# Attention weights normalised before they are transposed, a sink as a score column, and full-size products in filters and values

## The chip, the cores and the metric

The kernel runs on one core of a Trainium2 chip. Its time is the device time of one execution, in microseconds. Inputs and output lie in the device's main memory (HBM). The engines of the core are TensorE (PE; its weight loads are listed apart as PEld), VectorE (DVE), ScalarE (ACT), GpSimd (POOL) and SyncE (SP, which issues most DMAs). Each engine runs its own instructions in the order that was fixed when the program was built, and waits where an operand isn't ready.

## The reference, cut to what matters

A first block (retention, mLSTM and a feed-forward network over 512 tokens of width 1024) is followed by four layers: a latent attention, a windowed attention with a sink, a layer of long convolutions, and a second latent attention. There are 512 tokens and 256 context tokens; the last layer gives no context output. The change touches the softmax of the three attentions, and the convolutions' filters:

```python
def dense_attend(q, k, v, scale):            # latent attention, 8 heads
    s = jnp.einsum('bqhd,bkhd->bhqk', q, k).astype(jnp.float32) * scale
    p = jax.nn.softmax(s, axis=-1).astype(v.dtype)
    return jnp.einsum('bhqk,bkhd->bqhd', p, v)
...
def sink_attend(scores, values, sink_l):     # windowed attention, 16 heads in 4 groups
    sink_col = jnp.broadcast_to(sink_l[None, :, :, None, None], scores[0].shape[:-1] + (1,))
    p = jax.nn.softmax(jnp.concatenate(scores + [sink_col], axis=-1), axis=-1)
...
    y_x = (o_x * jax.nn.silu(gate_x)) @ w_out
...
def hyena_filters(n, f_w1, f_b1, f_freq, f_w2, f_b2, f_w3):
    h = jnp.sin(freq * (z @ f_w1 + f_b1))
    h = jnp.sin(freq * (h @ f_w2 + f_b2))
    h = (h @ f_w3).astype(jnp.float32).reshape(n, 2, C_ORDER, C_WIDTH)
    return h * jnp.exp(-t[:, :, None, None] * deltas)
```

## The kernel before, in words

All tensors lie with features on the 128 partitions and tokens along the columns. Precision beyond one pass of TensorE comes from splitting: `split` (line 396) writes a rounded high part with ScalarE and the remainder, the low part, with VectorE, and `mac` (line 436) multiplies high by high, high by low and low by high into one PSUM bank. Three products therefore stand for one.

The text of the kernel is a set of Python generators, which `weave` and `mix` interleave by given weights. That gives the written order; each engine's own order, fixed at build time, follows it closely, but takes an instruction ahead where an earlier one would wait. Tiles come from pools with a fixed number of buffers: four PSUM banks (`mm`), two double banks (`mm2`), eight tiles of 768 columns for softmax weights and other things (`P`), four of each small tag. A tile's next user waits for its last reader.

**The softmax** (line 1376) runs with queries on the partitions. VectorE takes the maximum of a row of scores in PSUM (line 1380), a one-column operation makes the exponential's bias of it (1382, or 1384 with the sink), ScalarE writes the exponentials `P` to SBUF and adds them up (1385), and VectorE takes the reciprocal of the sum into a column of `rd` (1389). With a sink, ScalarE also takes the sink's exponential (1387), which is added to the sum (1388). `P` stays unnormalised. The scale of the scores is a factor of the exponential.

**The latent attention** (`mla`) makes for each head 4 score tiles of 128 queries by 768 keys (`stageA`, line 1570), and in its first layer also 2 tiles of 128 context queries by 256 context keys. `stageB` (line 1590) goes over the blocks of 128 keys: `transposed` (line 1391) turns the block of all query tiles on TensorE (line 1395), splits the result, and `mac` multiplies it with the values one block later. At the end `over_columns` (line 1369) transposes each column of `rd`, broadcast to 128 columns, against the identity, so that 1/sum stands along the columns on all partitions (line 1373); VectorE multiplies it with the gate (1605) and with the output (1606). While `stageB` of one head runs, `stageA` of the next one and the preparation of later heads are woven in.

**The windowed attention** (`swa`) has 24 units (4 groups of heads; 2 context and 4 token tiles each). A unit's `stageA` (line 1703) makes the scores of its 4 heads: context keys, and a band of 2 or 3 blocks on which a mask is added by a product. `stageB` of the unit before is mixed in. Its values are stored with their high and low parts side by side, 64 columns each; `transposed` gives the weights' parts. A product of all 128 columns with the high weights (line 1739) gives two halves of the result, and one of the 64 high columns with the low weights (1738 or 1741) adds to the first half. ScalarE copies the transposed 1/sum with the factor 0.5 (1744), VectorE multiplies (1745), adds the two halves (1749) and applies the gate (1752).

**The filters** (`filter_unit`, line 1855) are made during the first block's feed-forward network (line 1156). The hidden layer `hv` has its high part in rows 0 to 63 and its low part in rows 64 to 127; the weights `w` repeat their high part in both halves. So line 1873 gives two of the three terms in one product with 128 rows; line 1874 adds the third with the 64 rows of the high part and the 64 rows of the low weights `l`. There are 48 such pairs.

**Queries**: `stacks` (line 1361) splits two halves of 64 rows so that high and low part of one head fill 128 rows; `split` does the same for the latent attention's 128-row queries.

Of the kernel before, what the change touches and what calls it, by code (L numbers as in the profile page):

```python
# [19 lines left out]
N = 512  # L20
# [234 lines left out]
class Kern:  # L255
# [140 lines left out]
    def split(self, dst, src):  # L396
        self.nc.scalar.copy(dst.hi, src)  # L397
        self.nc.vector.tensor_tensor(dst.lo, src, dst.hi.bitcast(F32), ALU.subtract)  # L398
# [962 lines left out]
    def stacks(self, r, n, d0, d1):  # L1361

        nc = self.nc
        nc.scalar.copy(d0[0:64, :], r[0:64, :])
        nc.vector.tensor_tensor(d0[64:128, :], r[0:64, :], d0[0:64, :].bitcast(F32), ALU.subtract)
        nc.scalar.copy(d1[64:128, :], r[64:128, :])
        nc.vector.tensor_tensor(d1[0:64, :], r[64:128, :], d1[64:128, :].bitcast(F32), ALU.subtract)
# [8 lines left out]
    def softmax(self, S, P, rd, scale, sink=None):  # L1376

        nc = self.nc
        s = self.sp.tile([128, 8], F32, tag="sm", name="sm")
        nc.vector.tensor_reduce(s[:, 0:1], S, AX.X, ALU.max)  # L1380
        if sink is None:
            nc.vector.tensor_scalar(s[:, 1:2], s[:, 0:1], -scale, None, ALU.mult)  # L1382
        else:
            nc.vector.tensor_scalar(s[:, 1:2], s[:, 0:1], -scale, sink[1], ALU.mult, ALU.min)
        nc.scalar.activation(P, S, AF.Exp, bias=s[:, 1:2], scale=scale, accum_out=s[:, 2:3])  # L1385
        if sink is not None:
            nc.scalar.activation(s[:, 3:4], sink[0], AF.Exp, bias=s[:, 1:2])
            nc.vector.tensor_tensor(s[:, 2:3], s[:, 2:3], s[:, 3:4], ALU.add)
        nc.vector.reciprocal(rd, s[:, 2:3])
# [48 lines left out]
    def mla(self, j, ctx_out, bg, end):  # L1438
# [107 lines left out]
        def queries(hp):  # L1546
            rp = self.wslot(4, 128)
            qs = [[self.b(dt=F32R), self.b(dt=F32R)], None]
            if ctx_out:
                t = self.b(dt=F32R)  # L1550
                qs[1] = [t[:, 0:256], t[:, 256:512]]
            for u in range(2):
                raw = self.wload(Wq, 0, 4, 384 * hp + 192 * u, 192)
                t = self.wslot(4, 128)
                self.split(rp[:, :, 64 * u:64 * u + 64], raw[:, :, 128:192])
                self.split(t, raw[:, :, 0:128])
                o = H[2 * hp + u]
                o["qs"] = [x[u] if x else None for x in qs]
                for i, n in ((0, N), (1, NC))[:2 if ctx_out else 1]:
                    q = self.bhl(n)  # L1560
                    self.split(q, self.proj([t[:, k, :] for k in range(4)], qn[i], n))
                    o["q"].append(q)
                yield
            rp = [rp[:, k, :] for k in range(4)]
            self.stacks(self.rope64(self.proj(rp, qn[0], N)), N, *qs[0])
            if ctx_out:
                self.stacks(self.proj(rp, qn[1], NC), NC, *qs[1])
            yield

        def stageA(h, i):  # L1570

            o = H[h]
            n = (N, NC)[i]
            o["P", i], o["rd", i] = [], self.sp.tile([128, 4], F32, tag="rd", name="rd")
            for qt in range(n // 128):
                sl = slice(128 * qt, 128 * qt + 128)
                ps = self.mm2() if i == 0 else self.mm()
                off = 256 if i == 0 else 0
                for x in (1, 0)[:2 - i]:
                    dst = ps[:, 512:1024] if x == 0 else ps[:, off:off + 256]  # L1580
                    self.mac(dst, [(o["q"][i][:, sl], o["k"][x])], stop=False)
                    nc.tensor.matmul(dst, o["qs"][i][:, sl], kr[x].hi, start=False, stop=False)  # L1582
                    nc.tensor.matmul(dst, o["qs"][i][:, sl], kr[x].lo, start=False, stop=True)  # L1583
                tot = 768 if i == 0 else 256
                P = self.P(tot)
                self.softmax(ps[:, off:off + tot], P, o["rd", i][:, qt:qt + 1], scale)
                o["P", i].append(P)
                yield

        def stageB(h, i):  # L1590
# [13 lines left out]
            rd = o["rd", i]  # L1604
            nc.vector.tensor_tensor(g, self.over_columns([rd[:, x:x + 1] for x in range(n // 128)], 128), g, ALU.mult)
# [23 lines left out]
    def swa(self, bg, end):  # L1629
# [5 lines left out]
        nsink = self.c2.tile([128, 16], F32, name="nsink")  # L1635
        nc.vector.tensor_scalar(nsink, self.sink, -1.0, None, ALU.mult)
# [32 lines left out]
        def queries(g, u, i):  # L1669
            def f(ps):  # L1670
# [6 lines left out]
                self.stacks(self.rope64(ps) if i == 0 else ps, ns[i], *gq[g, i][2 * u:2 * u + 2])  # L1677
# [25 lines left out]
        def stageA(g, i, qt):  # L1703
# [4 lines left out]
            rd = self.sp.tile([128, 4], F32, tag="rd", name="rd")  # L1708
            for v in range(4):
                ps = self.mm2()  # L1710
                q = gq[g, i][v][:, sl]
# [13 lines left out]
            U[g, i, qt] = (Ps, rd, list(range(k0, k1)) + [4, 5], sl)  # L1725

        def stageB(g, i, qt):
            Ps, rd, blocks, sl = U.pop((g, i, qt))
# [17 lines left out]
            ov = rb.rearrange("p (h q) -> p h q", h=4)  # L1746
            o = self.t(256)
            for v in range(2):
                nc.vector.tensor_tensor(o[64 * v:64 * v + 64, :].rearrange("p (h q) -> p h q", h=2), ov[0:64, v::2, :], ov[64:128, v::2, :], ALU.add)
            yield  # L1750
            for u in range(2):
                nc.vector.tensor_tensor(o[:, 128 * u:128 * u + 128], o[:, 128 * u:128 * u + 128], gs[g, i][u][:, sl], ALU.mult)
# [8 lines left out]
        def attend(some):  # L1761

            for x in some:
                n = units.index(x)
                prev = units[n - 1] if n else None
                yield from mix((stageA(*x), 4), (stageB(*prev), len(U[prev][2]) + 2) if prev else (None, 1))
# [68 lines left out]
    def filter_head(self, cg, o):  # L1835
# [8 lines left out]
        for op in (ALU.add, ALU.subtract):  # L1844
# [7 lines left out]
            ws.append((w, l[0:64, :]))  # L1852
        return dl, ws

    def filter_unit(self, cg, o, dl, ws):

        nc, I = self.nc, self.I
        for i, nt in ((0, 2), (1, 1)):
            hv = self.fh[i].rearrange("p (t q) -> p q t", q=2)
            for wi, (w, l) in enumerate(ws):  # L1860
# [8 lines left out]
                for par in range(2):  # L1869
                    for t in range(nt):  # L1870
# [3 lines left out]
                        nc.tensor.matmul(ps, x[0:64, :], l, start=False, stop=True)  # L1874
# [231 lines left out]
```

## Time and profile before

| | |
|---|---|
| time, median of 3 runs | 2917.35 us (2915.61 to 2918.12) |
| profiled execution: its own time / span of its instructions | 2918.76 us / 2917.0 us |
| granted clock of TensorE, mean over the span | 0.982 of full |
| TensorE busy (matmuls) | 2787.1 us, 96% |
| VectorE, ScalarE, GpSimd busy | 1814.9, 1334.4, 128.8 us |
| instructions | 44103, of them 17106 matmuls |

Busy time is the union of an engine's instructions. Matmuls overlap in their records, so a matmul's recorded length (some 0.39 us for 512 columns) is longer than the distance to the next one's start. A row of the view by group gives the line of the kernel, the engine and operation, what is written and read, the shape, the count, then the busy time and the mean length in ns, and behind the last bar the idle time before these instructions with what ended it. In the view in order of time a row gives the start and the length in us; "xN" merges neighbours of one kind.

### The profile page before, as it was taken

The numbers are of one execution on the slowest core, as the hardware profiler recorded it, in microseconds if no ns is written. First come the engines' busy times: TensorE is split into PE (matmuls) and PEld (weight loads), VectorE is DVE, ScalarE is ACT, GpSimd is POOL, SyncE is SP. The second block draws the span as 40 slices with busy tenths as digits, with TensorE's granted clock in tenths as the row PEclk, the third lists the DMA queues.
The fourth block names the chain that finished last, engine by engine and source line by source line (L and its number), as shares of the span: only waits on it lengthen the run. The fifth ranks groups of instructions, "written<-read, shape, count | busy, mean of one in ns | idle before, by whom it ended". The sixth has DMA issues, their size and how long they took to land. (4 is left out here: it accounts for less than half of the span.)

```text
span 2917.0 us, 44103 instructions
## 1 busy us (share of the span) xinstructions
PE 2787.1 (96%) x17106; PEld 2364.2 (81%) x17106; DVE 1814.9 (62%) x3775; ACT 1334.4 (46%) x2610; POOL 128.8 (4%) x158
## 2 busy tenths in 40 slices
PE   7999999999999999999999999989999998999998
PEld 4888878887777787888889877778888886887887
DVE  6665455555655556246768577788576777754774
ACT  4344344346455433345555566675332223544553
POOL 1000000000000000000000000000021122000000
PEclk8999999999999999999999999999999999999998
DMA  7233232544555536321234241123132226432122
GB/s 264 86 111 123 73 101 84 168 154 141 164 158 163 170 112 209 108 67 44 68 93 156 64 131 42 35 71 117 62 95 84 84 80 195 130 97 63 56 82 69
DMA packets 365830, 318.98 MB, mean 109 GB/s; under 512 B 17511, under 2 KB 326517, under 8 KB 365620
## 3 DMA queue, kind: packets, MB, share of 16 engines
q1 hardware_dynamic: 365204, 315.99, 35.2%
q8 instruction: 134, 2.20, 0.3%
q14 instruction: 76, 0.62, 0.1%
q0 software_dynamic: 416, 0.17, 0.0%
HBM read 273.90 MB, written 42.21 MB: 108 GB/s over the span
## 5 line engine op out<-in xcount | busy, mean ns | idle before, releaser
L441 PE MATMUL mm<-b,whi 128*128 128x512 f32 (+1 forms) x2548 | 895.8, 352 | 4.7 <-ACT whi L397 2.5
L443 PE MATMUL mm<-b,wlo 128*128 128x512 f32 (+1 forms) x2548 | 887.3, 348 | 1.2 <-DVE wlo L398 1.1
L442 PE MATMUL mm<-b,whi 128*128 128x512 f32 (+1 forms) x2548 | 887.6, 348 | 0.0
L441 PEld LDWEIGHTS mm<-b,whi 128*128 128x128 f32 x2548 | 486.1, 191 | 74.4 <-issue 5.8
L443 PEld LDWEIGHTS mm<-b,wlo 128*128 128x128 f32 x2548 | 486.1, 191 | 62.0 <-DVE wlo L398 2.3
L442 PEld LDWEIGHTS mm<-b,whi 128*128 128x128 f32 x2548 | 486.5, 191 | 60.2 <-issue 0.8
L398 DVE TENSOR_TENSOR wlo<-raw,whi 128x1024 fp32r<-128x1024 f32 (+3 forms) x286 | 292.0, 1023 | 239.7 <-ACT whi L397 224.1
L397 ACT CAST whi<-raw 128x1024 fp32r<-128x1024 f32 (+3 forms) x286 | 252.3, 885 | 397.1 <-PE mm L442 253.9
L443 PE MATMUL mm<-b 128*128 128x256 f32 (+1 forms) x628 | 189.4, 302 | 0.5 <-DVE b L398 0.3
L1385 ACT ACTIVATE P<-mm,sm 128x768 f32<-128x768 f32 (+3 forms) x176 | 127.9, 727 | 116.6 <-DVE sm L1382 68.4
L441 PE MATMUL mm<-b 128*128 128x256 f32 (+1 forms) x500 | 158.2, 318 | 8.4 <-ACT P L1385 4.6
L441 PE MATMUL mm<-b,P 128*128 128x256 f32 x560 | 161.8, 289 | 4.0 <-ACT b L575 2.8
L442 PE MATMUL mm<-b,P 128*128 128x256 f32 x560 | 160.4, 286 | 0.9 <-DVE b L576 0.8
L442 PE MATMUL mm<-b 128*128 128x256 f32 (+1 forms) x500 | 153.0, 307 | 0.4 <-DVE b L398 0.3
L1380 DVE TENSOR_REDUCE sm<-mm 128x1 f32<-128x768 f32 (+3 forms) x176 | 128.6, 733 | 39.7 <-PE mm L1583 23.8
L245 POOL TENSOR_TENSOR rs<-rs,mhalf 128x2 f32<-128x2 f32 (+1 forms) x44 | 42.3, 962 | 2427.2 <-DVE rs L244 2279.8
L398 DVE TENSOR_TENSOR t<-mm,t 128x512 fp32r<-128x512 f32 (+1 forms) x208 | 136.5, 663 | 15.3 <-ACT t L397 14.1
L397 ACT CAST t<-mm 128x512 fp32r<-128x512 f32 (+1 forms) x208 | 116.0, 569 | 54.8 <-PE mm L1395 51.6
L235 DVE TENSOR_TENSOR t<-t 128x256 f32<-128x256 f32 (+1 forms) x216 | 92.5, 441 | 71.9 <-ACT t L231 69.4
L1395 PE MATMUL mm<-ct,P 128*128 128x128 f32 x768 | 122.8, 276 | 13.0 <-ACT P L1385 8.2
L231 ACT ACTIVATE t<-b 128x256 f32<-128x256 f32 (+1 forms) x252 | 100.7, 431 | 67.7 <-DVE b L1101 40.9
L443 PEld LDWEIGHTS mm<-b 128*128 128x128 f32 x628 | 120.6, 192 | 5.6 <-DVE b L398 1.3
(351 smaller groups left out, 5129.7 us busy)
## 6 DMA issues: line engine op xcount, KB each, us to landing
raw<-in_w_mod_dram SPq DMA_DIRECT2D x96, 512.0 KB, 4.4
raw<-in_w_ada_dram SPq DMA_DIRECT2D x48, 512.0 KB, 3.9
raw<-in_w_in_dram SPq DMA_DIRECT2D x48, 512.0 KB, 4.0
raw<-in_w_ffn_in_dram SPq DMA_DIRECT2D x44, 512.0 KB, 4.1
raw<-in_c_w_in_dram SPq DMA_DIRECT2D x32, 512.0 KB, 4.3
raw<-in_a_w_in_dram SPq DMA_DIRECT2D x28, 512.0 KB, 4.1
ks<-t SPq DMA_DIRECT2D x48, 256.0 KB, 2.8
raw<-ks SPq DMA_DIRECT2D x24, 512.0 KB, 3.3
```

The costliest lines, as they stand in the source:

```text
L231: self.k.nc.scalar.activation(sq, x, AF.Square)
L235: self.k.nc.vector.tensor_tensor(self.acc, self.acc, sq, ALU.add)
L245: nc.gpsimd.tensor_tensor(s[:, 4:4 + nt], s[:, :nt], self.k.mhalf[:, :nt], ALU.pow)
L397: self.nc.scalar.copy(dst.hi, src)
L398: self.nc.vector.tensor_tensor(dst.lo, src, dst.hi.bitcast(F32), ALU.subtract)
L441: nc.tensor.matmul(ps, l.hi, r.hi, start=start and i == 0, stop=False)
L442: nc.tensor.matmul(ps, l.hi, r.lo, start=False, stop=False)
L443: nc.tensor.matmul(ps, l.lo, r.hi, start=False, stop=stop and i == n - 1)
L1380: nc.vector.tensor_reduce(s[:, 0:1], S, AX.X, ALU.max)
L1385: nc.scalar.activation(P, S, AF.Exp, bias=s[:, 1:2], scale=scale, accum_out=s[:, 2:3])
L1395: self.nc.tensor.transpose(ps[:, 128 * i:128 * i + 128], b, self.ident)
```

## The change

The softmax's weights are multiplied by 1/sum on GpSimd, in place, before they are transposed; `rd`, the transposes of its columns and the multiplications behind them go. The scale is multiplied into the queries when they are split. The sink becomes one more column of the scores, written into PSUM by ScalarE ahead of the head's score products, so that maximum, exponential and sum take it in; the column isn't transposed. In the windowed attention the low weights are multiplied with all 128 columns of the values. In the filters the low weights get 64 rows of zeros, and the product takes all 128 rows.

```diff
-    def split(self, dst, src):
-        self.nc.scalar.copy(dst.hi, src)
-        self.nc.vector.tensor_tensor(dst.lo, src, dst.hi.bitcast(F32), ALU.subtract)
+    def split(self, dst, src, scale=None):
...
+            nc.scalar.activation(dst.hi, src, AF.Copy, scale=scale)
+            nc.vector.scalar_tensor_tensor(dst.lo, src, scale, dst.hi.bitcast(F32), ALU.mult, ALU.subtract)
...
-    def softmax(self, S, P, rd, scale, sink=None):
+    def softmax(self, S, P, keep):
         nc = self.nc
-        s = self.sp.tile([128, 8], F32, tag="sm", name="sm")
-        nc.vector.tensor_reduce(s[:, 0:1], S, AX.X, ALU.max)
-        if sink is None:
-            nc.vector.tensor_scalar(s[:, 1:2], s[:, 0:1], -scale, None, ALU.mult)
-        else:
-            nc.vector.tensor_scalar(s[:, 1:2], s[:, 0:1], -scale, sink[1], ALU.mult, ALU.min)
-        nc.scalar.activation(P, S, AF.Exp, bias=s[:, 1:2], scale=scale, accum_out=s[:, 2:3])
-        if sink is not None:
-            nc.scalar.activation(s[:, 3:4], sink[0], AF.Exp, bias=s[:, 1:2])
-            nc.vector.tensor_tensor(s[:, 2:3], s[:, 2:3], s[:, 3:4], ALU.add)
-        nc.vector.reciprocal(rd, s[:, 2:3])
+        s = self.sp.tile([128, 4], F32, tag="sm", name="sm")
+        nc.vector.tensor_reduce(s[:, 0:1], S, AX.X, ALU.max, negate=True)
+        nc.scalar.activation(P, S, AF.Exp, bias=s[:, 0:1], accum_out=s[:, 1:2])
+        nc.vector.reciprocal(s[:, 2:3], s[:, 1:2])
+        nc.gpsimd.tensor_scalar(P[:, :keep], P[:, :keep], s[:, 2:3], None, ALU.mult)
...
-            rd = o["rd", i]
-            nc.vector.tensor_tensor(g, self.over_columns([rd[:, x:x + 1] for x in range(n // 128)], 128), g, ALU.mult)
             nc.vector.tensor_tensor(g, out, g, ALU.mult)
...
+                h = 4 * g + v
+                nc.scalar.copy(ps[:, 768:769], self.sink[:, h:h + 1])
...
-                P = self.P(nb + 256)
-                h = 4 * g + v
-                self.softmax(ps[:, 512 - nb:768], P, rd[:, v:v + 1], scale, (self.sink[:, h:h + 1], nsink[:, h:h + 1]))
+                P = self.P(nb + 257)
+                self.softmax(ps[:, 512 - nb:769], P, nb + 256)
...
-                    last = z == nb + LS - 1
-                    if last:
-                        nc.tensor.matmul(out[:64, :], v[:, g, 0], p.lo, start=False, stop=False)
-                    nc.tensor.matmul(out, v[:, g], p.hi, start=z == LS, stop=last)
-                    if not last:
-                        nc.tensor.matmul(out[:64, :], v[:, g, 0], p.lo, start=False, stop=False)
+                    nc.tensor.matmul(out, v[:, g], p.hi, start=z == LS, stop=False)
+                    nc.tensor.matmul(out, v[:, g], p.lo, start=False, stop=z == nb + LS - 1)
...
-            nc.scalar.activation(rb, self.over_columns([rd[:, x:x + 1] for x in range(4)], 128), AF.Copy, scale=0.5)
-            nc.vector.tensor_tensor(rb, out, rb, ALU.mult)
+            nc.scalar.copy(rb[64:128, :], out[64:128, :])
...
+            nc.gpsimd.memset(l[64:128, :].bitcast(F32), 0.0)
...
-                        nc.tensor.matmul(ps, x[0:64, :], l, start=False, stop=True)
+                        nc.tensor.matmul(ps, x, l, start=False, stop=True)
```

Left out here: the halves are added from `out` and `rb`, the factor 0.5 goes into the gate's multiplication, `nsink` goes, and `stacks` calls `split` with the scale.

## Rows read from the trace of the kernel before

**Rows 1.** Page, busy us of each engine (share of the span), instructions:
```profile
PE 2787.1 (96%) x17106; PEld 2364.2 (81%) x17106; DVE 1814.9 (62%) x3775; ACT 1334.4 (46%) x2610; POOL 128.8 (4%) x158
```
**Rows 2.** Busy time by stretch, each engine's us and count:
```profile
core 0: us, PE busy (x) PEld busy (x) DVE busy (x) ACT busy (x) POOL busy (x), PEclk, DMA share, GB/s
650.00:1005.00 355.00, 355.00 (x1620) 267.09 (x1619) 200.40 (x296) 189.87 (x256) 0.00 (x0) 1.00 0.52 162
1280.00:1520.00 240.00, 229.92 (x1429) 199.52 (x1428) 159.58 (x353) 130.46 (x285) 0.00 (x0) 0.99 0.21 65
1640.00:1995.00 355.00, 323.41 (x2066) 271.48 (x2065) 268.32 (x729) 220.78 (x547) 0.80 (x1) 0.98 0.24 72
2680.00:2855.00 175.00, 172.05 (x991) 145.82 (x990) 121.99 (x235) 98.04 (x195) 0.00 (x0) 0.98 0.21 64
```
**Rows 3.** Groups of TensorE's matmuls by line and shape:
```profile
L1739 PE MATMUL mm<-t,b 128*128 128x512 f32 x88 | 40.3, 458 | 3.6 <-ACT t L397 3.2 <-DVE t L398 0.3
...
L1373 PE MATMUL mm<-ct,rd 128*128 128x128 f32 x176 | 28.6, 279 | 0.0
...
L1874 PE MATMUL mm<-b 64*128 64x512 f32 x48 | 24.0, 500 | 0.0
```
**Rows 4.** TensorE in order of time, around a filter pair:
```profile
666.78 0.39 PE L443 MATMUL mm<-b,wlo 128*128 128x512 f32 x1
667.01 0.40 PE L1873 MATMUL mm<-b 128*128 128x512 f32 x1
667.34 0.50 PE L1874 MATMUL mm<-b 64*128 64x512 f32 x1
667.77 0.50 PE L441 MATMUL mm<-P,b 128*128 128x512 f32 x1
668.10 0.39 PE L442 MATMUL mm<-P,b 128*128 128x512 f32 x1
```
**Rows 5.** Group of the weight loads of line 1874:
```profile
L1874 PEld LDWEIGHTS mm<-b 64*128 64x128 f32 x48 | 9.1, 190 | 14.6 <-issue 14.6
```
**Rows 6.** TensorE in order of time, in the windowed attention:
```profile
1762.14 0.39 PE L1739 MATMUL mm<-t,b 128*128 128x512 f32 x1
1762.43 0.45 PE L1741 MATMUL mm<-t,b 128*64 128x512 f32 x1
1762.72 0.40 PE L1713 MATMUL mm<-b 128*128 128x256 f32 x2
...
1779.72 0.40 PE L1738 MATMUL mm<-t,b 128*64 128x512 f32 x1
1779.95 0.40 PE L1739 MATMUL mm<-t,b 128*128 128x512 f32 x1
1780.19 0.60 PE L1373 MATMUL mm<-ct,rd 128*128 128x128 f32 x4
1780.62 0.27 PE L1395 MATMUL mm<-ct,P 128*128 128x128 f32 x1
```
**Rows 7.** All engines in order of time, at a hand-over in the second latent attention:
```profile
2732.56 0.19 ACT L1385 ACTIVATION_READ_ACCUMULATOR P<-mm,sm 128x1 f32 x1
2732.81 0.33 PE L1395 MATMUL mm<-ct,P 128*128 128x128 f32 x1
...
2732.95 0.15 DVE L1389 RECIPROCAL rd<-sm 128x1 f32<-128x1 f32 x1
```
**Rows 8.** Group of GpSimd's additions in the convolutions:
```profile
L1995 POOL TENSOR_TENSOR t<-t 128x256 f32<-128x256 f32 x32 | 24.5, 766 | 298.0 <-DVE t L1994 255.4 <-issue 42.4
```
**Rows 9.** Groups of VectorE by line and shape:
```profile
L398 DVE TENSOR_TENSOR b<-t,b 128x512 fp32r<-128x512 f32 x100 | 68.2, 689 | 28.8 <-ACT b L397 28.2
...
L398 DVE TENSOR_TENSOR b<-t,P 128x512 fp32r<-128x512 f32 x32 | 29.2, 914 | 27.3 <-ACT P L397 26.8
...
L1384 DVE TENSOR_SCALAR sm<-sm,nsink 128x1 f32<-128x1 f32 x96 | 19.5, 207 | 1.1
...
L1745 DVE TENSOR_TENSOR t<-mm,t 128x512 f32<-128x512 f32 x24 | 16.6, 690 | 4.8 <-PE mm L1739 2.6 <-ACT t L1744 0.8 <-ACT P L1385 0.8
```
**Rows 10.** Group of ScalarE's exponentials of the sink:
```profile
L1387 ACT ACTIVATE sm<-sink,sm 128x1 f32<-128x1 f32 x96 | 27.6, 288 | 1.1 <-DVE sm L1384 1.0
```

More of the change, by code (lines that the diff above doesn't have):

```diff
@@ L394, in actf @@
         return out[:kt]
-    def split(self, dst, src):
-        self.nc.scalar.copy(dst.hi, src)
-        self.nc.vector.tensor_tensor(dst.lo, src, dst.hi.bitcast(F32), ALU.subtract)
+    def split(self, dst, src, scale=None):
+        nc = self.nc
+        if scale is None:
+            nc.scalar.copy(dst.hi, src)
+            nc.vector.tensor_tensor(dst.lo, src, dst.hi.bitcast(F32), ALU.subtract)
+        else:
+            nc.scalar.activation(dst.hi, src, AF.Copy, scale=scale)
+            nc.vector.scalar_tensor_tensor(dst.lo, src, scale, dst.hi.bitcast(F32), ALU.mult, ALU.subtract)
     def wload(self, W, r0, kt, c0, n):
@@ L1359, in rope64, with stacks @@
         return a
[L1361 to L1367, printed above, removed]
+    def stacks(self, r, n, d0, d1, scale):
+        for d, h, l in ((d0, slice(0, 64), slice(64, 128)), (d1, slice(64, 128), slice(0, 64))):
+            self.split(HL(d[h, :], d[l, :]), r[h, :], scale)
     def over_columns(self, cols, m):
@@ L1560, in queries @@
                     q = self.bhl(n)
-                    self.split(q, self.proj([t[:, k, :] for k in range(4)], qn[i], n))
+                    self.split(q, self.proj([t[:, k, :] for k in range(4)], qn[i], n), scale)
                     o["q"].append(q)
@@ L1564, in queries @@
             rp = [rp[:, k, :] for k in range(4)]
-            self.stacks(self.rope64(self.proj(rp, qn[0], N)), N, *qs[0])
+            self.stacks(self.rope64(self.proj(rp, qn[0], N)), N, *qs[0], scale)
             if ctx_out:
-                self.stacks(self.proj(rp, qn[1], NC), NC, *qs[1])
+                self.stacks(self.proj(rp, qn[1], NC), NC, *qs[1], scale)
             yield
@@ L1573, in stageA @@
             n = (N, NC)[i]
-            o["P", i], o["rd", i] = [], self.sp.tile([128, 4], F32, tag="rd", name="rd")
+            o["P", i] = []
             for qt in range(n // 128):
@@ L1585, in stageA @@
                 P = self.P(tot)
-                self.softmax(ps[:, off:off + tot], P, o["rd", i][:, qt:qt + 1], scale)
+                self.softmax(ps[:, off:off + tot], P, tot)
                 o["P", i].append(P)
@@ L1634, in swa @@
         self.axial()
-        nsink = self.c2.tile([128, 16], F32, name="nsink")
-        nc.vector.tensor_scalar(nsink, self.sink, -1.0, None, ALU.mult)
         V, ks, gq, gs = [], {}, {}, {}
@@ L1676, in f @@
                         gq[g, i] = [q[0][:, 0:256], q[0][:, 256:512], q[1][:, 0:256], q[1][:, 256:512]]
-                self.stacks(self.rope64(ps) if i == 0 else ps, ns[i], *gq[g, i][2 * u:2 * u + 2])
+                self.stacks(self.rope64(ps) if i == 0 else ps, ns[i], *gq[g, i][2 * u:2 * u + 2], scale)
             return f
@@ L1719, in stageA @@
                         nc.tensor.matmul(band, q, ks[0, g][z][:, 128 * k0:128 * k1], start=False, stop=z == 1)
-                P = self.P(nb + 256)
-                h = 4 * g + v
-                self.softmax(ps[:, 512 - nb:768], P, rd[:, v:v + 1], scale, (self.sink[:, h:h + 1], nsink[:, h:h + 1]))
+                P = self.P(nb + 257)
+                self.softmax(ps[:, 512 - nb:769], P, nb + 256)
                 Ps.append(P)
                 yield
-            U[g, i, qt] = (Ps, rd, list(range(k0, k1)) + [4, 5], sl)
+            U[g, i, qt] = (Ps, list(range(k0, k1)) + [4, 5], sl)
         def stageB(g, i, qt):
-            Ps, rd, blocks, sl = U.pop((g, i, qt))
+            Ps, blocks, sl = U.pop((g, i, qt))
             out = self.mm()
@@ L1735, in stageB @@
                     v, p = V[blocks[z - LS]], pt.pop(0)
-                    last = z == nb + LS - 1
-                    if last:
-                        nc.tensor.matmul(out[:64, :], v[:, g, 0], p.lo, start=False, stop=False)
-                    nc.tensor.matmul(out, v[:, g], p.hi, start=z == LS, stop=last)
-                    if not last:
-                        nc.tensor.matmul(out[:64, :], v[:, g, 0], p.lo, start=False, stop=False)
+                    nc.tensor.matmul(out, v[:, g], p.hi, start=z == LS, stop=False)
+                    nc.tensor.matmul(out, v[:, g], p.lo, start=False, stop=z == nb + LS - 1)
                 yield
             rb = self.t()
-            nc.scalar.activation(rb, self.over_columns([rd[:, x:x + 1] for x in range(4)], 128), AF.Copy, scale=0.5)
-            nc.vector.tensor_tensor(rb, out, rb, ALU.mult)
-            ov = rb.rearrange("p (h q) -> p h q", h=4)
+            nc.scalar.copy(rb[64:128, :], out[64:128, :])
+            ov = [x.rearrange("p (h q) -> p h q", h=4) for x in (out[0:64, :], rb[64:128, :])]
             o = self.t(256)
             for v in range(2):
-                nc.vector.tensor_tensor(o[64 * v:64 * v + 64, :].rearrange("p (h q) -> p h q", h=2), ov[0:64, v::2, :], ov[64:128, v::2, :], ALU.add)
+                nc.vector.tensor_tensor(o[64 * v:64 * v + 64, :].rearrange("p (h q) -> p h q", h=2), ov[0][:, v::2, :], ov[1][:, v::2, :], ALU.add)
             yield
             for u in range(2):
-                nc.vector.tensor_tensor(o[:, 128 * u:128 * u + 128], o[:, 128 * u:128 * u + 128], gs[g, i][u][:, sl], ALU.mult)
+                nc.vector.scalar_tensor_tensor(o[:, 128 * u:128 * u + 128], o[:, 128 * u:128 * u + 128], 0.5, gs[g, i][u][:, sl], ALU.mult, ALU.mult)
                 if g < 3:
@@ L1765, in attend @@
                 prev = units[n - 1] if n else None
-                yield from mix((stageA(*x), 4), (stageB(*prev), len(U[prev][2]) + 2) if prev else (None, 1))
+                yield from mix((stageA(*x), 4), (stageB(*prev), len(U[prev][1]) + 2) if prev else (None, 1))
         weave((dense(0, WB - 2), 6))
@@ L1851, in filter_head @@
             nc.scalar.copy(w[64:128, :], w[0:64, :].bitcast(F32))
-            ws.append((w, l[0:64, :]))
+            nc.gpsimd.memset(l[64:128, :].bitcast(F32), 0.0)
+            ws.append((w, l))
         return dl, ws
```

1 line of the change is left out of this document (removed).

## The prediction

> **What bounds the kernel now.** I read the page first: TensorE's matmuls are busy 2787.1 us of a span of 2917.0 us, all other engines 62% or less [rows 1]. That is an average over stages, so the second view is the busy time by stretch [rows 2]. The changed lines lie in four. In 650 to 1005 us, where the filters are woven into the feed-forward products, TensorE has no idle time at all: 355.00 of 355.00. In the first latent attention (1280 to 1520) it idles 10.1 us, in the second (2680 to 2855) 3.0 us. In the windowed attention (1640 to 1995) it idles 31.6 us, with VectorE busy 268.3. So a microsecond that TensorE no longer spends is a microsecond of the span in the first stretch, nearly one in the latent attentions, and less sure in the windowed one. "Busy" hides waste, though: matmuls overlap in their records, so what one costs is the distance from its start to the next start. That is the third view, the order in time on TensorE [rows 4, 6].
>
> **Filters (line 1874 from 64 to 128 rows).** A plain product over 512 columns takes 0.23 us from start to start (666.78 to 667.01). The 128-row product before a 64-row one takes 0.33, the 64-row one 0.43, and the first product after it 0.33: 1.09 us from 667.01 to 668.10 where three plain products take 0.69 [rows 4]. The reason stands in the weight loads: all 48 loads of line 1874 have idle time before them put down to "issue", 14.6 us together [rows 5]: they are not loaded under the product before. 0.40 us for each of the 48 pairs [rows 3] is 19.2 us, on an engine without idle time. The added clearing of the other 64 rows (two per filter, eight in all) is GpSimd work in a stretch in which GpSimd does nothing [rows 2], done with the weights well ahead of the products: 0; without that lead the first product of a filter would wait for it.
> The Trainium skill, "TensorEngine Tiling (Array Packing)", Key Properties, says that changing the tiling mode drains TensorE. By that rule too the cost goes with the mixing of shapes; the trace agrees with its 0.33, 0.43 and 0.33. The skill's "TensorE: Matmul & The Clock Gate", Why this matters for your kernels, says on the contrary that a single product with K=32 takes the same time as with K=128; by it alone this edit would be worth 0. Here the 0.43 decides against it, but it is the third rival below.
>
> **The transposes of 1/sum.** 176 go [rows 3]: 40 groups of four (8 heads in each latent attention, 24 units of the windowed one) and 8 of two (context queries of the first). A group of four takes 0.43 us until the next start (1780.19 to 1780.62) [rows 6]; half of it for two: 40 x 0.43 + 8 x 0.215 = 18.9 us. With each group go a PSUM bank and a pass over it on VectorE or ScalarE.
>
> **Values (lines 1738 to 1741 from 64 to 128 columns).** 88 pairs [rows 3]. In the middle of an accumulation a pair takes 0.29 + 0.29, where two plain products take 0.46: 0.12 lost; at its end, with the small one first, 0.23 + 0.24: 0.01 lost [rows 6]. Between 1 and 10.6 us; I take the middle, 0.06 x 88 = 5 us.
>
> **Small work on VectorE and ScalarE.** In the windowed attention VectorE loses 96 one-column operations of line 1384 (19.5 us) and 24 passes of line 1745 (16.6 us) [rows 9], and as many one-column sums as exponentials of the sink. It has 86.7 us free there, so this counts only where TensorE waits for it: at most the 31.6 us of idle time; I take 4. ScalarE gives up 96 exponentials of the sink (27.6 us) [rows 10] and gets 96 one-column copies in front of the score products. TensorE's first product into that bank may wait for the copy, and behind it queue the other heads' products; the copy costs between 0 and the 288 ns of the old exponential, so 0 to 27.6 us. I take +2, since most copies should find their bank free early. The scale put into the queries' split changes a copy into a copy with a factor and a subtraction into one with a factor, on passes of the same size: 0.
>
> **The multiplication on GpSimd.** This is the price. The weights now go to the transposes only after the reciprocal on VectorE and one GpSimd pass. Before, at a hand-over (where a unit's last weights meet its first transposes) in the second latent attention, the sum is read at 2732.56 to 2732.75, the last transpose starts at 2732.81 and the reciprocal at 2732.95 to 2733.10, needed by nobody yet [rows 7]. Now the reciprocal (its end 0.35 us after the sum's) stands in the path, then the pass. GpSimd's nearest row has two inputs: 766 ns for 256 columns [rows 8], which is 2.30 us for 768. The lowest price is VectorE's rate, 689 ns for 512 [rows 9], 1.03 us for 768. I take 1.6, between them, because it is the same slow engine with one input fewer. With the operation between maximum and exponential gone (0.2 us, line 1384) [rows 9], weights are ready some 1.2 to 2.5 us later, about 1.8. All of it counts only where the transposes are the next thing TensorE could do. There are 48 such hand-overs (24 units, 16 in the first and 8 in the second latent attention). Behind a waiting transpose everything of TensorE's order waits, the next head's scores among it. But this order is set when the program is built, and the idle time in the latent stretches, 13.1 us in 415, says that other products usually fill such waits. So I count a sixth, 0.3 us x 48 = +14 us; the ends are 0 and 48 x 1.8 = 86 us.
> GpSimd and VectorE also slow each other: the same subtraction over 512 columns takes 914 ns on average behind GpSimd's output, and 689 elsewhere [rows 9]. VectorE has room for that in all four stretches [rows 2]; it only adds to the upper end of the hand-over.
> The Trainium skill, "SBUF — State Buffer", Who interferes with whom, calls the port pair that the two share an exclusive lock. By that a multiplication that meets a 0.69 us subtraction begins up to 0.69 us later, at most 33 us over 48 hand-overs, and the sum below would come to about 2 us slower. The 914 ns agree that they collide, and not how often they will.
>
> **Sum.** -19.2 - 18.9 - 5 - 4 + 2 + 14 = -31 us. The profiled execution took 2918.76 us, 1.4 more than the median of 2917.35, so 2918.8 - 31 = 2887.7, or 2886 on the median's scale; I write 2887, between them.
>
> **Rivals.**
> First, the hand-overs cost nothing, because enough scores of the next head stand ahead of every transpose: the 14 us fall away, 2872. For it speaks 172.05 us busy of 175 [rows 2]; against it, that the transpose of 2732.81 starts 0.06 us after its sum was read, so this order has no reserve [rows 7].
> Second, the other side: the multiplication lies open at every hand-over. It costs 86 us against 45 gained: 2917 + 41 = 2958. It decides from 45/48 = 0.94 us for each hand-over; above that the kernel is slower. For it speaks the same missing reserve, and GpSimd's rate of 3 ns per column; against it, that this needs TensorE to find nothing else 48 times.
> Third, the filter edit gives nothing, because what is slow is not the 64 rows but reading new weights there, which stays: 2887 + 19 = 2906. Against it: the 128-row load of line 1873 after a plain product starts on time, 0.23 us after it [rows 4]. The skill's K=32 rule, cited above, would have it so.
>
> **How the numbers follow.** Forecast 0.52, first rival 0.24, second 0.10, third 0.14. The range goes down to 2862 (hand-overs free, the 10.6 us for the values, a little more of the idle time) and up to 2916 (hand-overs at 0.9 us each); beyond that lie the second rival and a little of the first. Within 0.2% (5.8 us), about what a measurement of this kernel can tell from no change, is hand-overs of 0.8 to 1.1 us each, or the third rival with hand-overs of 0.4 to 0.7: 0.07. Slower: 0.09, nearly all of the second rival. Faster: 0.84.
>
> **What would show it.** Lines 1873 and 1874 both at 0.23 us from start to start, no "issue" time before their weight loads, and the stretch from the first to the last of them some 19 us shorter: the filter step. Line 1373 without the 176: the transposes. TensorE idle before the transposes with GpSimd as releaser: more than 14 us there moves towards the second rival, none towards the first. GpSimd's passes over 768 columns outside 1.03 to 2.30 us make the price wrong. TensorE waiting for the sink's copy by more than 2 us in the windowed attention makes that term wrong. A total above 2912 would mean that the hand-overs or the third rival ate the gain; below 2862, that VectorE held the windowed attention more than its free time suggests.

## The result, and the profile after

The kernel became slower: 2931.6 us in the median (2928.3 to 2937.5) against 2916.5 for the kernel before on the same chip, a ratio of 1.0055 (95% interval 1.0036 to 1.0074). The forecast was 2887. The profiled execution has a span of 2928.3 us and took 2930.1.

The page: busy us of each engine, answering to [rows 1]. TensorE does 26.7 us less work and is idle 38 us longer; GpSimd works 310 us more.
```profile
PE 2760.4 (94%) x16930; PEld 2354.7 (80%) x16930; DVE 1762.3 (60%) x3454; ACT 1330.8 (45%) x2610; POOL 438.3 (15%) x342
```
Busy time by stretch, as in [rows 2]; the stages have moved by up to 15 us, and the last stretch is 10 us longer.
```profile
650.00:1005.00 355.00, 351.98 (x1677) 278.41 (x1675) 205.79 (x303) 196.33 (x264) 3.13 (x6) 1.00 0.54 168
1280.00:1520.00 240.00, 216.17 (x1292) 186.50 (x1291) 139.89 (x269) 121.47 (x262) 86.22 (x48) 0.96 0.20 62
1640.00:1995.00 355.00, 319.65 (x1994) 270.95 (x1993) 236.93 (x517) 218.98 (x552) 146.51 (x97) 0.97 0.24 71
2680.00:2865.00 185.00, 167.90 (x934) 139.57 (x934) 116.16 (x196) 96.91 (x191) 70.70 (x32) 0.97 0.19 58
```
In the first latent attention TensorE is idle 23.8 us of 240 where it was 10.1, in the second 17.1 of 185 where it was 3.0 of 175. What it waits for there stands in the view of waits: TensorE's line and what released it, then us in total, times, and the longest. In the order of the first latent, the windowed and the second latent attention:
```profile
PE mm L1391 <- POOL P L1385: 21.6, 12, 3.0
...
PE mm L1391 <- POOL P L1385: 11.6, 18, 1.5
...
PE mm L1391 <- POOL P L1385: 15.1, 10, 4.4
```
All three are the transposes (line 1391 now) that wait for the multiplication (1385) on GpSimd. Its groups by shape:
```profile
L1385 POOL TENSOR_SCALAR P<-P,sm 128x768 f32<-128x768 f32 x64 | 143.5, 2244 | 315.3 <-DVE sm L1384 305.4 <-PE mm L1391 9.9
...
L1385 POOL TENSOR_SCALAR P<-P,sm 128x512 f32<-128x512 f32 x32 | 52.3, 1639 | 54.0 <-DVE sm L1384 38.9 <-PE mm L1391 5.9 <-PE mm L446 4.4
...
L1385 POOL TENSOR_SCALAR P<-P,sm 128x256 f32<-128x256 f32 x48 | 46.8, 979 | 113.7 <-DVE sm L1384 100.2 <-ACT b L1655 6.1 <-ACT b L402 5.9
```
A pass over 768 columns takes 2.24 us; the line through 979 and 2244 ns is 2.47 ns for a column and 0.35 us for each pass. The filters went as forecast. TensorE around a pair, at the place of [rows 4], is evenly spaced at 0.23 us, and the weight loads of [rows 5] have no "issue" time left:
```profile
666.68 0.39 PE L1863 MATMUL mm<-b 128*128 128x512 f32 x1
666.91 0.40 PE L1864 MATMUL mm<-b 128*128 128x512 f32 x1
667.14 0.39 PE L446 MATMUL mm<-P,b 128*128 128x512 f32 x1
```
```profile
L1864 PEld LDWEIGHTS mm<-b 128*128 128x128 f32 x48 | 9.3, 194 | 1.5
```
A hand-over in the second latent attention, all engines in order of time, answering to [rows 7]:
```profile
2732.39 0.19 ACT L1383 ACTIVATION_READ_ACCUMULATOR P<-mm,sm 128x1 f32 x1
2732.62 0.16 DVE L1384 RECIPROCAL sm<-sm 128x1 f32<-128x1 f32 x1 [0.46 <-ACT P L1383]
2732.88 2.21 POOL L1385 TENSOR_SCALAR P<-P,sm 128x768 f32<-128x768 f32 x1 [1.92 <-DVE sm L1384]
...
2735.14 0.33 PE L1391 MATMUL mm<-ct,P 128*128 128x128 f32 x1 [1.41 <-POOL P L1385]
```
Before, 0.25 us lay between the reading of the sum and the transpose; now 2.75 do, and TensorE stands still for 1.41 of them. In the first latent attention the biggest waits, eight of 2.1 to 2.6 us and one of 3.3 between two starts on TensorE (the expectations below count nine of 2.1 to 2.6), stand elsewhere: at the context tiles, whose own pass takes 0.92 us. In eight of the nine this pass begins right behind one of 768 columns. One of them, engine by engine:
```profile
1331.37 3.11 POOL L1385 TENSOR_SCALAR P<-P,sm 128x768 f32<-128x768 f32 x2 [2.07 <-DVE sm L1384]
```
```profile
1331.85 0.15 DVE L1384 RECIPROCAL sm<-sm 128x1 f32<-128x1 f32 x1
```
```profile
1331.96 0.38 PE L1391 MATMUL mm<-ct,P 128*128 128x128 f32 x2
1332.09 0.36 PE L446 MATMUL mm<-b 128*128 128x256 f32 x1
1334.53 0.44 PE L1391 MATMUL mm<-ct,P 128*128 128x128 f32 x2 [2.08 <-POOL P L1385]
```
The context tile's reciprocal ends at 1332.00, but GpSimd began a pass of 768 columns at 1331.37, for the next head, which nobody needs yet. The 256 columns are the second half of that row ("x2", 3.11 us).

### The profile page after: what moved, and what is told of

It reads as the page before. It is cut to its first block, busy times and chain, and to the rows that moved or that the text cites. A ratio compares the mean times of both kernels' runs of the same rounds, so it can differ in the third digit from the quotient of the medians.

```text
span 2928.3 us, 43869 instructions
## 1 busy us (share of the span) xinstructions
PE 2760.4 (94%) x16930; PEld 2354.7 (80%) x16930; DVE 1762.3 (60%) x3454; ACT 1330.8 (45%) x2610; POOL 438.3 (15%) x342
## 5 line engine op out<-in xcount | busy, mean ns | idle before, releaser
L1385 POOL TENSOR_SCALAR P<-P,sm 128x768 f32<-128x768 f32 (+3 forms) x176 | 304.7, 1737 | 547.8 <-DVE sm L1384 502.7
L1391 PE MATMUL mm<-ct,P 128*128 128x128 f32 x768 | 129.4, 282 | 51.5 <-POOL P L1385 48.3
L1382 DVE TENSOR_REDUCE sm<-mm 128x1 f32<-128x768 f32 (+4 forms) x176 | 128.5, 734 | 70.1 <-PE mm L1579 37.0
L1383 ACT ACTIVATE P<-mm,sm 128x768 f32<-128x768 f32 (+4 forms) x176 | 128.3, 730 | 93.2 <-DVE sm L1382 91.8
L1391 PEld LDWEIGHTS mm<-ct,P 128*128 128x128 f32 x768 | 94.2, 143 | 79.8 <-POOL P L1385 59.5
```

The source lines that it names most:

```text
L1382: nc.vector.tensor_reduce(s[:, 0:1], S, AX.X, ALU.max, negate=True)
L1383: nc.scalar.activation(P, S, AF.Exp, bias=s[:, 0:1], accum_out=s[:, 1:2])
L1385: nc.gpsimd.tensor_scalar(P[:, :keep], P[:, :keep], s[:, 2:3], None, ALU.mult)
L1391: self.nc.tensor.transpose(ps[:, 128 * i:128 * i + 128], b, self.ident)
```

## Experiments

Most kernels start from the changed one. A table of stages carries the verdicts: from the first score product of a stage to the start of its last transposes, in us, worked out from TensorE's rows in one profiled execution of each kernel. Stages that an edit leaves alone still differ by up to 3 us (e1, which touches none of the three, has 232.0, 337.4 and 171.9), so smaller differences say nothing.

| kernel | first latent | windowed | second latent | time, us | ratio to before |
|---|---|---|---|---|---|
| before | 230.3 | 335.6 | 175.0 | | 1 |
| changed | 247.4 | 331.4 | 186.9 | 2931.6 | 1.0055 |
| e2, pass after its readers | 221.0 | 325.6 | 167.1 | 2892.4 | 0.9910 |
| e3, no multiplication | 221.2 | 316.6 | 167.6 | 2871.7 | 0.9834 |
| e4, all on VectorE | 229.0 | 328.7 | 172.5 | 2896.4 | 0.9918 |
| e5, last tiles on VectorE | 239.2 | 323.9 | 175.8 | 2899.0 | 0.9942 |
| e6, old normalisation | 226.4 | 327.5 | 170.4 | 2891.5 | 0.9909 |
| e7, scores first | 249.4 | 331.1 | 181.2 | 2925.2 | 1.0031 |
| e10, early scores | 253.8 | 326.6 | 174.7 | 2922.4 | 1.0016 |
| e12, e6 and early scores | 225.3 | 321.5 | 170.6 | 2879.3 | 0.9872 |
| e14, context passes on VectorE | 231.6 | 331.8 | 185.1 | 2913.7 | 0.9982 |
| e15, long passes on VectorE | 231.7 | 330.1 | 187.6 | 2914.3 | 0.9982 |
| e16, first block first | 250.1 | 332.2 | 176.4 | 2927.4 | 1.0035 |

**e1, the filters alone**, on the kernel before:
```diff
+            nc.gpsimd.memset(l[64:128, :].bitcast(F32), 0.0)
...
-                        nc.tensor.matmul(ps, x[0:64, :], l, start=False, stop=True)
+                        nc.tensor.matmul(ps, x, l, start=False, stop=True)
```


> The kernel before with the filter edit alone (64 rows of zeros, products of 128 rows). The changed kernel's last filter pair came 13.2 us earlier than the kernel before's. Theory (the gain was real and was lost later): 2916.5 - 14 = 2902, between 2896 and 2905. Rival (the filters only moved ahead, and the time was never won): 2913 to 2920.

2903.5 us, 0.9945 (0.9933 to 0.9958): 16 us, for 19.2 forecast. The third rival falls.

**e2, the load without the wait.** GpSimd makes passes of the same number and sizes, by a constant, behind the last transposes that read the tile; the weights stay unnormalised.
```diff
-        nc.gpsimd.tensor_scalar(P[:, :keep], P[:, :keep], s[:, 2:3], None, ALU.mult)
...
+                        nc.gpsimd.tensor_scalar(P[:, :128 * nkb], P[:, :128 * nkb], 0.5, None, ALU.mult)
...
```
(The same stands in the windowed attention.)

> The changed kernel with GpSimd's pass over the weights, by a constant, moved behind the last transpose that reads them, so that nobody but the buffer's next user waits for it; the output is not normalised. Theory (the waits of the transposes cost the time): close to e3, within 8 us, so 2870 to 2890. Rival (GpSimd's work itself costs, by collisions with VectorE and by holding the weights' buffers): close to the changed kernel, 2920 to 2935.

**e3, no multiplication**: the line goes, and the weights stay unnormalised.

> The changed kernel without the multiplication on GpSimd; the output is not normalised. Theory (the hand-overs cost some 50 us): 2931.6 - 50 = 2880, between 2872 and 2890, with the idle time of TensorE in the latent attentions back at 10 and 3 us. Rival (the sink's copy, the fuller products or the order of the work cost the time): over 2905.

2892.4 (0.9894 to 0.9926), 2 us above its theory's range and 21 above e3 where at most 8 were expected, and 2871.7 (0.9819 to 0.9848), just under the lower end of its own. Both latent attentions of e2 are as short as those of e3: there GpSimd's work costs nothing unless somebody waits for it. The windowed one is 9 us longer even so, and another 7 us lie in e2's end. Much of this is e2's own doing. Its late passes hold the `P` tiles, which ScalarE and VectorE want for the parts of the next weight matrices; so in the windowed attention the adding of a unit's two halves (line 1743) comes late, and TensorE, released by it, waits 5.72 us once where it waits 1.21 in e3:
```profile
1953.61 0.62 ACT L399 CAST P<-raw 128x512 fp32r<-128x512 f32 x1 [2.93 <-POOL P L1731]
...
1957.09 0.77 PE L1735 MATMUL mm<-t,b 128*128 128x512 f32 x1 [5.72 <-DVE t L1743]
```
Behind the second latent attention it's the same: four late passes, from 2815.00 to 2823.42, hold such tiles, and TensorE waits 2.49 and 1.81 us for parts that e3 has in time.

The price of the multiplication is the changed kernel against e3: 26 us in the first latent attention, 15 in the windowed, 19 in the second; by the ratios 0.0221 x 2917 = 64 us in all.

**e4, all on VectorE**, and **e5, only a unit's last tile there** (48 of 176):
```diff
-        nc.gpsimd.tensor_scalar(P[:, :keep], P[:, :keep], s[:, 2:3], None, ALU.mult)
+        (nc.vector if last else nc.gpsimd).tensor_scalar(P[:, :keep], P[:, :keep], s[:, 2:3], None, ALU.mult)
```
(These are e5's lines; in e4 it is `nc.vector` throughout.)

> The changed kernel with the multiplication on VectorE instead of GpSimd. A pass over 768 columns should take some 0.95 us there in place of 2.24. Theory (it is the length of the pass at the hand-overs): some 25 us faster than the changed kernel, 2900 to 2912. Rival (any product between exponential and transposes costs the same, by the wait itself): 2925 or more.

> The changed kernel, but the multiplication of a unit's last tile of weights (48 of them) is on VectorE; the other 144 stay on GpSimd. Theory (the time is lost at the hand-over, where the last tile's GpSimd pass of some 2.2 us is all that the first transposes wait for): about the time of the kernel with every multiplication on VectorE, 2885 to 2900, and TensorE's waits for GpSimd before the transposes almost gone. Rival (GpSimd as an engine is too slow for the whole unit, so its passes queue, and the next to last tile is late too): only part of the loss comes back, 2905 to 2925, and the waits stay with GpSimd as releaser.

2896.4 (0.9905 to 0.9931), 4 us better than expected, and 2899.0 (0.9928 to 0.9956). VectorE takes 618 ns for 768 columns, not the 950 of the expectation, in e4's groups:
```profile
L1385 DVE TENSOR_SCALAR P<-P,sm 128x768 f32<-128x768 f32 x64 | 39.6, 618 | 1.9
```
Even so e4 lies 25 us above e3, 12 of them in the windowed attention. e5 gets back half of the price and lies in its theory's range, but the waits for GpSimd are not almost gone: 19.6 us of the 48 (21.6, 11.6 and 15.1) are left. The first latent attention keeps 18 us over e3. Of its eight waits over 1 us there, five are for 256-column passes on GpSimd, and four of these passes begin right behind one of 768: the rival's queue is part of it.

**e6, the old normalisation** (`rd`, its 176 transposes and the multiplications behind the products are back; all else of the change stays).
```diff
-        nc.vector.reciprocal(s[:, 2:3], s[:, 1:2])
-        nc.gpsimd.tensor_scalar(P[:, :keep], P[:, :keep], s[:, 2:3], None, ALU.mult)
+        nc.vector.reciprocal(rd, s[:, 1:2])
```


> The changed kernel with the old normalisation: the columns of 1/sum are transposed again (176) and multiplied behind the products; scale in the queries, sink as a column, full-size values and filters stay. Theory (the transposes of 1/sum cost some 19 us, and the multiplication on GpSimd some 60): 2871.7 + 19 to 25, so 2889 to 2897, about 40 us faster than the changed kernel. Rival (the transposes of 1/sum filled gaps of TensorE, so that dropping them gave less than 8 us): 2872 to 2880.

2891.5 (0.9895 to 0.9924), as the theory had it. Against e3 the transposes and passes of 1/sum cost 20 us.

**e7, the next head's scores first**, and **e8, that with e5**:
```diff
-            weave((b, nb), (a, 4), p)
+            weave((a, 4), (b, nb), p)
```
(In the first latent attention both also leave one step empty between the context's scores and their transposes.)

> The changed kernel with another written order in the latent attentions: the next head's score tile is put ahead of the transposes that wait for GpSimd, where before the transposes stood first. Theory (a hand-over costs what of the pass isn't covered by products written ahead of the transposes): MLA stretches 15 to 30 us shorter, 2900 to 2916. Rival (the order on TensorE already takes products ahead as far as their banks and operands are ready, or the next scores wait for a bank that is held by the same chain): no change, 2926 to 2936.

> The last tile's multiplication on VectorE, and the next head's score tile ahead of the transposes in the latent attentions. Theory (both act on the same wait): little below the kernel with the last tile alone on VectorE, 0 to 8 us faster than it, 2880 to 2895. Rival (the order acts by itself): the two gains add, 15 us or more below it.

2925.2 (1.0019 to 1.0042) and 2903.4 (0.9945 to 0.9971). e7 is 6 us better than the changed kernel and ends just under its rival's range; e8 is 4 us worse than e5, outside both. In both comparisons the intervals overlap. One place in the written order is no cover to speak of.

**e10 to e13, early scores**: the next unit's four score tiles are through when two thirds of the unit before are; with GpSimd, with VectorE, with the old normalisation, without multiplication.
```diff
-            weave((b, nb), (a, 4), p)
+            weave((b, nb), (a, 4.8 if two else 6), p)
...
-                yield from mix((stageA(*x), 4), ...
+                yield from mix((stageA(*x), 6), ...
```
(`nb` is 16 in the first latent attention, and was 11.)

> The changed kernel, all multiplications on GpSimd, but with the next unit's four score tiles written earlier: they end when about two thirds of the unit before is done (before: three quarters or more), so that transposes and products of the unit before lie between the last score tile and the transposes that need it, in both latent attentions and the windowed one. Theory (a hand-over costs what of 0.35 + 2.24 us isn't covered by work written ahead of it): the waits for GpSimd fall to less than half, 2885 to 2905. Rival (GpSimd's four passes of a unit in a row, 9 us, are the limit, wherever the tiles stand, or the softmax then waits for banks): 2920 to 2940.

> The same early score tiles, with every multiplication on VectorE (618 ns for 768 columns there). Theory (the 25 us by which the kernel with VectorE lies above the one without multiplication are the rest of the same wait): 2873 to 2885. Rival (they are VectorE's own load in the softmax's chain, which no order hides): 2892 to 2900.

> The same early score tiles with the old normalisation behind the products. Control for the order: here nothing between exponential and transposes can be hidden that was there in the kernel with the old normalisation (2891.5). If the early order acts on the multiplication's wait alone, 2888 to 2895; if it is a better or worse order by itself, outside of that.

> The same early score tiles without the multiplication (the weights stay unnormalised). Floor for this order: 2866 to 2874 if the order acts on the multiplication alone (2871.7 in the old order). The distance from the kernel with GpSimd in the same order is what the multiplication costs when it is covered: theory under 25 us, rival 50 us or more as in the old order (60).

2922.4 (1.0006 to 1.0027), 2887.8 (0.9883 to 0.9910), 2879.3 (0.9857 to 0.9887) and 2868.0 (0.9814 to 0.9841). As a whole the theory of cover fell: with GpSimd the multiplication still costs 54 us (2922.4 - 2868.0). By stages it holds in one and fails in another. In the second latent attention TensorE's wait for GpSimd fell from 15.1 to 6.8 us, and the stage is 12 us shorter; in the first it rose from 21.6 to 24.7, and the stage is 6 us longer. The view of waits of e10, second latent attention, then first:
```profile
PE mm L1391 <- POOL P L1385: 6.8, 7, 1.4
...
PE mm L1391 <- POOL P L1385: 24.7, 17, 3.1
```
e11 ended between its two ranges. e12 lies below the range for an order that acts on the multiplication alone: with the old normalisation the order helps too. e13 lies inside its range, only 4 us below e3: without any normalisation the order gives next to nothing. e12 is the fastest kernel of this study that does all of the reference's work.

**e14 and e15, who stands in the queue.** In the first latent attention alone, e14 puts the 16 context passes on VectorE, e15 the 32 long ones:
```diff
+        (nc.vector if vec else nc.gpsimd).tensor_scalar(P[:, :keep], P[:, :keep], s[:, 2:3], None, ALU.mult)
...
+                self.softmax(ps[:, off:off + tot], P, tot, ctx_out and i == 1)     # e15: i == 0
```


> The changed kernel; only the first latent attention's context tiles (16 passes of 256 columns, 0.92 us each on GpSimd) are multiplied on VectorE. Theory (queue: these passes stand on GpSimd behind a pass of 768 columns for the next head, which nobody needs yet; TensorE's nine waits of 2.1 to 2.6 us there are mostly that): 15 to 20 us off the changed kernel, 2911 to 2917. Rival (a hand-over costs the own pass): 8 x (0.92 - 0.35) = 5 us off, 2925 to 2930.

> The reverse in the first latent attention: the 32 passes of 768 columns are on VectorE, the context tiles' passes stay on GpSimd. Theory (queue): the context tiles' passes begin as soon as their reciprocal is there, and nearly all of the 26 us that the multiplication costs in this stage go but for the own passes (8 x 0.9 at most): 2908 to 2916. Rival (the own pass of the context tile is what TensorE waits for): the nine waits stay at 2 us, 2924 to 2932.

2913.7 (0.9971 to 0.9992) and 2914.3 (0.9973 to 0.9992): the two opposite edits take the same 16 us out of the same stage. In e15 the context tile still goes to GpSimd at the place shown above; its pass now starts 0.17 us after the reciprocal's end, and TensorE waits 0.5 us instead of 2.08:
```profile
1332.86 0.15 DVE L1384 RECIPROCAL sm<-sm 128x1 f32<-128x1 f32 x1
1333.18 0.93 POOL L1385 TENSOR_SCALAR P<-P,sm 128x256 f32<-128x256 f32 x1 [3.42 <-DVE sm L1384]
...
1334.16 0.44 PE L1391 MATMUL mm<-ct,P 128*128 128x128 f32 x2 [0.50 <-POOL P L1385]
```
So most of that stage's price is the queue, not the pass that TensorE waits for.

**e16, the first block first**: each pass is cut after the 128 columns that the first transposes read.
```diff
-        nc.gpsimd.tensor_scalar(P[:, :keep], P[:, :keep], s[:, 2:3], None, ALU.mult)
+        for a, b in ((0, 128), (128, keep)):
+            nc.gpsimd.tensor_scalar(P[:, a:b], P[:, a:b], s[:, 2:3], None, ALU.mult)
```


> The changed kernel with every multiplication in two: the first 128 columns, which the unit's first transposes read, and then the rest. Theory (in the second latent attention and the windowed one TensorE waits for the length of the last tile's pass, 1.6 to 2.2 us): the first part takes some 0.66 us by the line through the measured lengths, so 1.5 us less at the 8 and some 1 us at the windowed hand-overs that wait, while the first latent attention's queue gets no shorter: 2912 to 2922. Rival (the wait is for the whole chain or GpSimd's total work, which grows by 176 x 0.35 us): 2930 to 2945.

2927.4 (1.0023 to 1.0047), between the two ranges. The second latent attention is 10.5 us shorter, and its wait falls from 15.1 to 8.8 us:
```profile
PE mm L1392 <- POOL P L1386: 8.8, 8, 2.9
```
There it was the length of the last pass. The windowed attention gained nothing, and doesn't decide the matter: TensorE waits there 26 times, 12.8 us in all, instead of 18 times, 11.6 us, and of the 18 waits over 0.25 us nine are now for the second part.

**e17, filters and early scores on the kernel before.**

> The kernel before with the filter edit and the early score tiles, the old normalisation, scale in the exponential, sink apart. It says how much of the 12 us between the two kernels with the old normalisation (2891.5 and 2879.3) the order gives by itself. If the order acts by itself: 2903.5 - 12, so 2888 to 2896. If it needs the shorter softmax of the change: 2900 to 2907.

2895.8 (0.9904 to 0.9933), 8 us below e1, inside the first range: most of the 12 us that e12 has over e6 come without the rest of the change.

## Why the prediction was wrong

By differences of the ratios, times 2917 us (each good to some 5 to 7 us):

| term | forecast | measured | from |
|---|---|---|---|
| filters | -19.2 | -16 | e1 to before |
| values, small work, sink copies | -7 | -10.5 | e6 to e1 |
| transposes of 1/sum | -18.9 | -22 | e3 to e6 |
| multiplication | +14 | +64 | changed to e3 |
| sum | -31 | +16 | |

The gains came nearly as forecast, 48 us where 45 stood, with the single terms off by 3 to 4 us in both directions, within what these differences can tell. **The step that failed is the one "So I count a sixth, 0.3 us x 48 = +14 us".** The measured price is 64/48 = 1.33 us for each hand-over where 0.3 stood, above the break-even of 0.94 that the second rival named. That rival is nearest to what happened, at 64 us instead of 86, but not at every hand-over: by stages, the changed kernel against e3, the price is 26/16 = 1.6 us in the first latent attention, 15/24 = 0.6 in the windowed and 19/8 = 2.4 in the second. Three things were wrong in the step.

First, the share. I read the small idle time of the latent stretches as a sign that other products fill such waits. It showed only that the chain of before was no longer than what stood ahead of it. [Rows 7] had the transpose 0.06 us after the sum was read: a chain with next to no reserve. Read in the same way, five of that stage's eight hand-overs have 0.05 or 0.06 us and three have 0.88, and the change adds 2.5 us; at the place shown above other products covered 1.1 of these, and 1.41 became a wait. I quoted the missing reserve against the first rival and did not let it count in the sum. e10 and e16 bear it out for the second latent attention: more cover, or a shorter pass, and 10 to 12 of its 19 us come back.

Second, what I left out: I named what queues behind the transpose on TensorE, and not what stands ahead of the pass on GpSimd. The pass that is needed starts behind one that is not. e14 and e15 take 16 of the 26 us out of the first latent attention in this way.

Third, the size. "I take 1.6" for 768 columns; 2.24 was measured, at the upper bound of 2.30 that came from a two-input row. The idea that one input fewer is faster found nothing: per column the one-input pass is no quicker than [rows 8] (979 ns for 256 columns, against 766). The Trainium skill, "GPSIMD Engine Reference", 4.1 Engine selection, has one-input work there at roughly line rate and only two-input work twice as slow as VectorE. The trace differs: 2244 ns against VectorE's 618 on the same tile, 3.6 times.

The collision of GpSimd and VectorE, for which up to 33 us stood beside the sum, shows little on VectorE: over 512 columns the subtraction of [rows 9] that took 689 ns takes 703, and in the windowed attention the low parts of the transposed blocks take 683 ns with the passes and 682 without (e3). On GpSimd 13 of the 176 passes are over 15% longer than the median of their width, all while VectorE ran two-input operations on SBUF, which fits a collision. One of 3.35 us, where 2.21 is usual, stands before the longest wait of all:
```profile
2848.93 3.35 POOL L1385 TENSOR_SCALAR P<-P,sm 128x768 f32<-128x768 f32 x1 [2.07 <-DVE sm L1384]
...
2852.34 0.69 PE L1391 MATMUL mm<-ct,P 128*128 128x128 f32 x2 [4.42 <-POOL P L1385]
```
The sink's copy: TensorE waited 3.0 us for it in the score products and 0.6 in others, so by the prediction's own sign the 2 us were too few.

The windowed attention's 15 us stay partly open. Against e3 TensorE idles 10 us longer there (34.5 us against 24.9) and takes 5 us longer for the same products (296.9 against 291.7). e2's 9 us are no measure of it, since half of them is the one wait shown above. The length of a pass alone isn't shown to be the cause: e16 only moved the waits, and e4, whose passes take about a third of the time but load VectorE, keeps 12 of the 15. What all these kernels share is the longer chain of each tile; a kernel that shortens this chain in the windowed attention alone wasn't tried.

## What to carry to other kernels

Before putting an operation between a producer and the engine that bounds the kernel, measure the reserve at that very place: from the producer's end to the consumer's start in order of time. An engine with no idle time can be one whose chain just fits, and then most of the addition counts. And on a slow engine count the queue: the pass that is urgent waits for the pass that is not, so give the urgent ones to a quick engine, or keep the correction behind the products, as e12 does (2879.3 us, 0.9872 of before, the fastest here that normalises).

## What was not expected of the hardware

A wait can cost more than its length. In the changed kernel TensorE idled 1.76 us before its start at 2833.51, waiting for a pass; from 2835.08 the same products over 512 columns stood 0.42 us apart instead of 0.23. The view by stretch puts the granted clock (the column after POOL's) at 1.00 over the wait and at 0.52 behind it, which is the lower level of 1.2 GHz:
```profile
2829.75:2834.85 5.10, 3.34 (x19) 2.37 (x17) 2.17 (x5) 1.97 (x4) 2.21 (x1) 1.00 0.66 206
2835.08:2838.63 3.55, 3.55 (x15) 2.87 (x13) 2.66 (x5) 3.10 (x7) 2.21 (x1) 0.52 0.22 61
```
Such a drop doesn't follow every wait: behind the one that ends at 1334.53, of 2.08 us, the granted clock is 1.00 over the next 6 us. In the first latent attention it is 0.96 in the changed kernel and 0.99 in e3; over 240 us that makes an estimate of 7 us of the stage's 26, and no row names a wait for them. The busy time agrees: the same 1347 products take 223.6 us there against 215.7. In the three stages together 18 of the 60 us lie in products that take longer, and 42 in idle time.

VectorE's multiplication by a column runs at 0.80 ns per column (618 ns for 768), its two-input subtraction at 1.35 (689 for 512, [rows 9]). The Trainium skill, "VectorE: DVE Perf Modes", The perf-mode tier table, gives a one-input fp32 operation in SBUF twice the rate of a two-input one. The trace agrees in the direction, at 1.7 times.
